# Nearest-neighbour upsampling on one core: two of the three loads move from SyncE to ScalarE

## The chip, the core and the metric

The kernel runs on one core of a Trainium2 chip. A core has several engines that run their own instruction streams and meet only through semaphores: TensorE, VectorE (DVE in the profile), ScalarE (ACT), GpSimd (POOL) and SyncE (SP). Data move between the chip's memory (HBM) and the core's own memory of 128 partitions by sixteen DMA engines. An engine issues a transfer, here SyncE or ScalarE, and the transfer's pieces are put on a hardware queue of that engine; the sixteen DMA engines work the queues off. In the profile q1 is the queue of SyncE and q10 that of ScalarE. The metric is the device time of one launch, in microseconds (us).

## The reference

The input `x` has 16 images of 64 channels of 64 x 64 floats (16.78 MB). Each pixel becomes a 2 x 2 block of the output, which has 16 x 64 x 128 x 128 floats (67.11 MB). Nothing is calculated; every number is copied four times.

```python
for i in range(new_h):
    for j in range(new_w):
        result[:, :, i, j] = x[:, :, i // scale_factor, j // scale_factor]
```

## The kernel before

All images and channels are laid end to end, which gives 65,536 rows of 64 floats. Each of the 128 partitions gets 512 consecutive rows, 128 KB. One tile, `mem`, holds a free part of 79 x 256 floats and behind it (from the index `WF` on) the 512 rows of the input, `xt`.

The input comes by three loads (line 195): rows 0 to 31, rows 32 to 287 and rows 288 to 511 of each partition, that is 8 KB, 64 KB and 56 KB in each partition, or 1024, 8192 and 7168 KB in all. Before the change all three are issued by SyncE, one after the other.

The output is made in nine groups of 54, 38, 54, 60, 54, 62, 64, 62 and 64 input rows. For each, VectorE copies the rows to a place in `mem` with each row twice and each float twice (`expanded`, line 215), and one DMA stores that place to HBM (line 217). The place alternates: even groups go to the start of `mem`, odd ones end where the group's own input rows begin, over input that is already used. A group can only be copied once the store that last read its place has landed. In the first group, row 0 is copied by an instruction of its own (line 214), which waits for the first load alone; the other 53 rows follow in a second copy, which waits for the second load. Groups 0, 1 and 8 are stored by SyncE, the others by ScalarE.

Semaphores and waits are put in by the framework. Two functions then edit the finished program. `begin_before_barrier` takes SyncE's first `EARLY` instructions out of the kernel's body, which must be loads that wait for nothing, and puts them into the opening part of the program, ahead of SyncE's first drain. That drain belongs to the opening barrier, at which all engines meet, so these loads start without waiting for the other engines. `close_early` edits the end: it lets GpSimd clear the semaphores early, and SyncE's last instruction waits for the last store. `close_on_gpsimd` is not used.

Of the kernel before, what the change touches and what calls it, by code (L numbers as in the profile page):

```python
# [6 lines left out]

EARLY = 3  # L10


def begin_before_barrier(nc):

    blocks = nc.main_func.blocks
    main, body = blocks[0], blocks[1]
    sp = mybir.EngineType.SP
    loads = [i for i in body.instructions if i.engine == sp][:EARLY]  # L20
    for load in loads:
        assert isinstance(load, mybir.InstDMACopy), type(load)
        assert not (load.sync_info and load.sync_info.on_wait)
    names = [i.name for i in loads]
    body.instructions = [i for i in body.instructions if i.name not in names]
    kept = list(main.instructions)
    at = next(
        n
        for n, i in enumerate(kept)
        if i.engine == sp and isinstance(i, mybir.InstDrain)  # L30
    )
    kept[at:at] = loads
    main.instructions = kept


def close_on_gpsimd(nc):
# [117 lines left out]
@with_exitstack  # L154
def kernel(
    ctx: ExitStack,
    tc: tile.TileContext,
    x: bass.AP,
    scale_factor: int,
    out: bass.AP,  # L160
):
    nc = tc.nc
    nc.at_finalize(begin_before_barrier)
    nc.at_finalize(close_early)
    P = nc.NUM_PARTITIONS
    s = int(scale_factor)
    B, C, H, W = x.shape
    R = B * C * H // P
    fdt = x.dtype

    xp = x.rearrange("b c h w -> (b c h) w").rearrange("(p r) w -> p r w", p=P)
    op = out.rearrange("b c (h hd) w -> (b c h) (hd w)", hd=s).rearrange(
        "(p r) w -> p r w", p=P
    )

    rows = [54, 38, 54, 60, 54, 62, 64, 62, 64]
    GROW = s * s
    FREE = 79
    WF = FREE * GROW * W
    assert sum(rows) == R
    mem_pool = ctx.enter_context(tc.tile_pool(name="mem", bufs=1))
    mem = mem_pool.tile([P, WF + R * W], fdt, name="mem")
    xt = mem[:, WF:].rearrange("p (r w) -> p r w", r=R)

    HEAD = 32
    cuts = [0, HEAD, R // 2 + HEAD, R]
    for lo, hi in zip(cuts, cuts[1:]):
        nc.sync.dma_start(out=xt[:, lo:hi], in_=xp[:, lo:hi])  # L195

    def expanded(r0, r1):
        return (
            xt[:, r0:r1].unsqueeze(2).unsqueeze(4).to_broadcast([P, r1 - r0, s, W, s])
        )  # L200

    r0 = 0
    before = (0, 0)
    for n, k in enumerate(rows):
        size = k * GROW * W
        at = 0 if n % 2 == 0 else WF + r0 * W - size
        assert at >= before[1] or at + size <= before[0]
        before = (at, at + size)
        u = mem[:, at : at + size].rearrange(
            "p (k a w b) -> p k a w b", k=k, a=s, w=W  # L210
        )
        k0 = 1 if n == 0 else 0
        if k0:
            nc.vector.tensor_copy(out=u[:, :k0], in_=expanded(r0, r0 + k0))  # L214
        nc.vector.tensor_copy(out=u[:, k0:], in_=expanded(r0 + k0, r0 + k))  # L215
        issuer = nc.sync if n in (0, 1, len(rows) - 1) else nc.scalar
        issuer.dma_start(out=op[:, r0 : r0 + k, :], in_=u)
        r0 += k
# [35 lines left out]
```

## Time and profile before

| | |
|---|---|
| time of the runs (median of 3) | 197.12 us (197.11 to 197.22) |
| span of the profiled execution, first to last instruction | 195.7 us |
| its own time, as far as the profile gives it | the span; the median of the runs is 1.4 us above it |
| VectorE busy | 76.9 us, 10 instructions |
| moved by DMA | 83.89 MB in 1728 packets |
| mean rate over the span | 429 GB/s |

The span counts from the first instruction to the last. A DMA is one instruction, but 144 packets here: eight rows of partitions and one small completion flag for each of the sixteen DMA engines, so that the 12 DMAs (three loads, nine stores) make 1728. A packet counts at its beginning in a view of short stretches, with all its bytes and all its time; in a stretch shorter than a packet, the DMA share and the rate can therefore be far above 1 and 430 or zero, while the mean over some packets is right. In the rows of such stretches stand: from and to, length, VectorE's busy time (with the number of instructions), GpSimd's, the TensorE clock, the DMA share and GB/s. Rows that begin with q1 or q10 give packets, MB and the share of the time of sixteen DMA engines. In the chain and in the timeline a row begins with start and duration in us. "SPq" and "ACTq" are the instructions by which SyncE and ScalarE issue, wait and meet at barriers.

### The profile page before, as it was taken

Reading aid. Unit: us, or ns where it says so; the run is one execution under the profiler, and the core shown is the slowest. Engines: PE = TensorE matmul, PEld = TensorE weight load, DVE = VectorE, ACT = ScalarE, POOL = GpSimd, SP = SyncE. Lnnn points to the kernel's source line nnn. Section 1 sums busy time; section 2 is a strip of 40 time slices with the busy share of each in tenths; the row PEclk is TensorE's granted clock in tenths of the full one; section 3 lists DMA queues with packets and bytes.
Section 4 is the critical chain, followed back from the end, with each engine's and each line's share of the span. In section 5 each row is a group of like instructions: output and inputs, shape, how many; then the busy total and the mean of one; then the engine's idle time right before and its main releaser. Section 6 shows DMA issues by size and latency. Waiting matters only on the chain.

```text
span 195.7 us, 76 instructions
## 1 busy us (share of the span) xinstructions
DVE 76.9 (39%) x10; POOL 0.2 (0%) x4
## 2 busy tenths in 40 slices
DVE  0000099990029287059008805920790079000000
POOL 0000000000000000000000000000000000000000
DMA  9999989989898988999999899999999999999994
GB/s 429 429 429 429 402 375 492 445 362 543 362 435 382 540 384 362 543 402 402 402 492 452 362 543 415 415 415 415 429 429 429 429 415 441 550 476 422 429 429 214
DMA packets 1728, 83.89 MB, mean 429 GB/s; under 512 B 192, under 2 KB 192, under 8 KB 192
## 3 DMA queue, kind: packets, MB, share of 16 engines
q10 hardware_dynamic: 864, 46.66, 55.0%
q1 hardware_dynamic: 864, 37.22, 44.3%
HBM read 16.78 MB, written 67.11 MB: 429 GB/s over the span
## 4 chain that ended last, share of the span: by engine, by line
DMA 61%; DVE 24%; SPq 0%; issue 0%
DMA out_dram<-mem 49%; DVE mem L215 24%; DMA mem<-in_x_dram 12%; SPq L195 0%
## 5 line engine op out<-in xcount | busy, mean ns | idle before, releaser
L215 DVE COPY mem<-mem 128x13824 f32<-128x13824 f32 (+5 forms) x9 | 76.6, 8515 | 84.6 <-DMA out_dram<-mem 65.5
L214 DVE COPY mem<-mem 128x256 f32<-128x256 f32 x1 | 0.3, 293 | 4.9 <-DMA mem<-in_x_dram 4.9
L235 POOL MEMSET const-bfloat16-1.0<- 128x1 bf16 x1 | 0.1, 101 | 0.0
L235 POOL MEMSET const-uint8-127<- 128x1 uint8 x1 | 0.1, 101 | 0.0
L235 POOL MEMSET const-float32-0.0<- 128x1 f32 x1 | 0.1, 98 | 0.2 <-issue 0.2
L235 POOL MEMSET const-float32-1.0<- 128x1 f32 x1 | 0.1, 98 | 0.0
## 6 DMA issues: line engine op xcount, KB each, us to landing
out_dram<-mem ACTq DMA_DIRECT2D x2, 7936.0 KB, 31.6
out_dram<-mem ACTq DMA_DIRECT2D x2, 6912.0 KB, 23.7
out_dram<-mem ACTq DMA_DIRECT2D x1, 7680.0 KB, 26.1
mem<-in_x_dram SPq DMA_DIRECT2D x1, 7168.0 KB, 40.2
out_dram<-mem SPq DMA_DIRECT2D x1, 6912.0 KB, 18.9
out_dram<-mem SPq DMA_DIRECT2D x1, 4864.0 KB, 25.1
mem<-in_x_dram SPq DMA_DIRECT2D x1, 1024.0 KB, 4.8
mem<-in_x_dram SPq DMA_DIRECT2D x1, 23.8
```

The lines of the kernel that those rows point to most:

```text
L214: nc.vector.tensor_copy(out=u[:, :k0], in_=expanded(r0, r0 + k0))
L215: nc.vector.tensor_copy(out=u[:, k0:], in_=expanded(r0 + k0, r0 + k))
L235: nc = _bacc.Bacc("TRN2", target_bir_lowering=False, num_devices=1)
```

## The change

The second and third load are issued by ScalarE instead of SyncE. `EARLY` becomes a table, one load for SyncE and two for ScalarE, and `begin_before_barrier` does for each of the two engines what it did for SyncE: it takes that many loads out of the body and puts them ahead of the engine's own drain in the opening part. Sizes, copies, stores and their queues, and the end of the program stay. The waits of copies and stores are on the same transfers as before.

```diff
-EARLY = 3
+EARLY = {mybir.EngineType.SP: 1, mybir.EngineType.Activation: 2}
...
     main, body = blocks[0], blocks[1]
-    sp = mybir.EngineType.SP
-    loads = [i for i in body.instructions if i.engine == sp][:EARLY]
-    for load in loads:
-        assert isinstance(load, mybir.InstDMACopy), type(load)
-        assert not (load.sync_info and load.sync_info.on_wait)
-    names = [i.name for i in loads]
-    body.instructions = [i for i in body.instructions if i.name not in names]
-    kept = list(main.instructions)
-    at = next(
-        n
-        for n, i in enumerate(kept)
-        if i.engine == sp and isinstance(i, mybir.InstDrain)
-    )
-    kept[at:at] = loads
-    main.instructions = kept
+    for engine, count in EARLY.items():
+        loads = [i for i in body.instructions if i.engine == engine][:count]
+        for load in loads:
+            assert isinstance(load, mybir.InstDMACopy), type(load)
+            assert not (load.sync_info and load.sync_info.on_wait)
+        names = [i.name for i in loads]
+        body.instructions = [i for i in body.instructions if i.name not in names]
+        kept = list(main.instructions)
+        at = next(
+            n
+            for n, i in enumerate(kept)
+            if i.engine == engine and isinstance(i, mybir.InstDrain)
+        )
+        kept[at:at] = loads
+        main.instructions = kept
...
     for lo, hi in zip(cuts, cuts[1:]):
-        nc.sync.dma_start(out=xt[:, lo:hi], in_=xp[:, lo:hi])
+        issuer = nc.scalar if lo else nc.sync
+        issuer.dma_start(out=xt[:, lo:hi], in_=xp[:, lo:hi])
```

## The prediction

> **What bounds the kernel now.** I read the page first, then the chain that ended last, then short stretches of the DMA traffic, since the page points there. Its queue part says that the two hardware queues, q1 (SyncE's) and q10 (ScalarE's), together took 55.0 + 44.3 = 99.3% of the time of all sixteen DMA engines over the span. VectorE, the only engine that computes, was busy for 39%.
>
> ```profile
> span 195.7 us, 76 instructions
> DVE 76.9 (39%) x10; POOL 0.2 (0%) x4
> q10 hardware_dynamic: 864, 46.66, 55.0%
> q1 hardware_dynamic: 864, 37.22, 44.3%
> HBM read 16.78 MB, written 67.11 MB: 429 GB/s over the span
> ```
>
> So the time is close to bytes over rate, and only a hole in the DMA traffic can lengthen it. The chain of waits shows where such a hole could come from: one load, the long first copy, the first store, and so on.
>
> ```profile
> 0.00 0.37 SPq L195
> 0.37 0.05 issue
> 0.42 23.76 DMA mem<-in_x_dram
> 24.19 0.02 issue
> 24.21 14.30 DVE mem L215
> 38.51 0.02 issue
> 38.52 18.93 DMA out_dram<-mem
> ```
>
> Call the three loads A (32 of the 512 image rows that a partition holds, 8 KB of it), B (256, 64 KB) and C (224, 56 KB), and the first store S0. B is seen landed at 24.2, VectorE copies until 38.5, S0 is issued at 38.52. Did the DMA engines run dry before S0? Packets are booked at the moment they begin and each DMA engine takes one partition's row at a time, so the traffic shows as waves of sixteen packets:
>
> ```profile
> 38.20:38.61 0.41, 0.38 (x2) 0.00 (x0) 1.00 5.18 2238
> 38.61:40.32 1.71, 1.71 (x1) 0.00 (x0) 1.00 0.00 0
> 40.32:40.73 0.41, 0.41 (x1) 0.00 (x0) 1.00 5.00 2158
> 40.73:42.36 1.63, 1.63 (x1) 0.00 (x0) 1.00 0.00 0
> 42.36:42.77 0.41, 0.41 (x1) 0.00 (x0) 1.00 4.98 2158
> ```
>
> The last column is GB/s booked. The wave at 38.20 is 2238 GB/s x 0.41 us = 0.92 MB, C's last rows (16 x 56 KB); the next at 40.32 is 0.88 MB, S0's first (16 x 54 KB). They are 2.12 us apart, and 0.92 MB / 2.12 us = 433 GB/s, the full rate: no hole. Two longer stretches, of one queue and of two, show nearly the same rate:
>
> ```profile
> 171.00:182.80 11.80, 0.00 (x0) 0.00 (x0) 1.00 0.99 428
> 58.00:68.00 10.00, 6.83 (x1) 0.00 (x0) 1.00 1.01 436
> ```
>
> **The change, part by part.** SyncE keeps A and loses two DMA issues; ScalarE gains those for B and C, ahead of its opening barrier. No byte, copy or store changes, nor which queue a store is on.
>
> *When B is issued.* Now it follows A on SyncE; then it is ScalarE's first work. The trace of before has ScalarE at its first instruction, the drain of the opening barrier, at 0.1 us.
>
> ```profile
> L235 ACTq DRAIN  x1: 8/8/8, 0.1 to 0.1; - x1
> L195 SPq DMA_DIRECT2D mem<-in_x_dram x3: 373/424/432, 0.0 to 0.9; - x3
> DMA to landing us min/median/max: 4.8/23.8/40.2
> 0.00 1.32 SPq L195 DMA_DIRECT2D mem<-in_x_dram  x3
> ```
>
> So B is issued at about 0.1 instead of 0.42, and C at about 0.1 + 0.42 + 0.05 = 0.6 instead of 0.9. That saves 0.3 us of issuing that lies on no path as long as A keeps the DMA engines busy: the engines start on A at 1.0, which is unchanged, and B only has to be there when they would run out.
>
> ```profile
> 0.50:1.00 0.50, 0.00 (x0) 0.00 (x0) 1.00 0.00 0
> 1.00:1.50 0.50, 0.00 (x0) 0.00 (x0) 1.00 1.97 279
> 1.50:2.00 0.50, 0.00 (x0) 0.00 (x0) 1.00 0.15 49
> 2.00:2.50 0.50, 0.00 (x0) 0.00 (x0) 1.00 0.89 360
> 4.00:4.50 0.50, 0.00 (x0) 0.00 (x0) 1.00 5.13 2212
> ```
>
> The burst at 4.00 to 4.50 is B's first wave (2212 x 0.5 = 1.1 MB), beginning as A's rows end. Term: 0.
>
> *The barrier.* SyncE reaches it 0.9 us sooner, ScalarE 0.9 us later (two issues of 0.42 to 0.43). What is behind it is VectorE's first copy, at 4.9 in before. Term: 0; the cover is over 3 us.
>
> *How A and B share the DMA engines.* This is the real content of the change. On one queue A went wholly ahead of B; on two queues they interleave. The trace shows how, where the last store (q1) joins the one before it (q10). First SyncE's store issues, the last of which ends at 38.52 + 128.19 = 166.71; then four stretches in order, each one wave long: 168.58 to 170.92, 170.92 to 173.33, 173.33 to 175.67, and 182.84 to 185.26.
>
> ```profile
> 38.52 128.19 SPq L217 DMA_DIRECT2D out_dram<-mem  x3
> ...
> q10 hardware_dynamic: 16, 1.02, 100.1%
> ...
> q1 hardware_dynamic: 16, 1.05, 100.3%
> ...
> q10 hardware_dynamic: 16, 1.02, 100.1%
> ...
> q1 hardware_dynamic: 16, 1.05, 100.0%
> q10 hardware_dynamic: 16, 0.00, 0.4%
> ```
>
> One row from one queue, one row from the other, at no loss of rate: 1.02 MB in 2.34 us is 436 GB/s. The last pair is the completion flags of q10 (16 packets of no size), which came only after one more wave of the other queue. Eight rows of A at 8 KB will then alternate with eight rows of B at 64 KB, and A, landed at 4.8 now, lands at about 21 to 24. The sum of A and B is the same, so B still lands at about 24.2. Only line 214's copy waits for A alone; it took 0.29 us.
>
> ```profile
> L214 DVE COPY mem<-mem 128x256 f32<-128x256 f32 x1 | 0.3, 293 | 4.9 <-DMA mem<-in_x_dram 4.9
> ```
>
> If A lands a wave ahead of B (A is issued first, and above, the wave of 168.58 is still q10's though the other store was issued by 166.71: an engine seems to have one more row of its current queue committed before it turns to the other), that copy stays hidden behind B's last wave. If they land together, it goes ahead of the long copy, which starts 0.29 + 0.02 = 0.31 us later, and S0 is issued at 38.83. S0's rows can begin 1.0 us after issue, as A's do on idle engines: 39.83, still before the engines finish C at 40.32. The slack is 40.32 - 38.52 - 1.00 = 0.80 us, so 0.31 costs nothing. Term: 0 either way; with the cover gone it would be the excess over 0.80.
>
> [...]
>
> *C beside the first stores.* C stays behind B on one queue. Now S0 queues behind C on q1; then it stands on another queue, and can alternate with C's last wave. C may land a wave (2 us) later. The first copy that reads its rows is the sixth of the nine, at 103.41, so nothing waits:
>
> ```profile
> 103.41 8.43 DVE L215 COPY mem<-mem 128x15872 f32<-128x15872 f32 x1 [10.83 <-DMA out_dram<-mem]
> ```
>
> SyncE's second store no longer has a load ahead of it either. From S0's landing on, the chain is the one of before. Term: 0.
>
> *The ramp.* This is the one unknown with a price. The first sixteen packets took long: 1.05 MB began at 1.0 and ended at 4.0 to 4.5, middle 4.25, where 1.05 MB / 434 GB/s = 2.4 us would do. The loss is 3.25 - 2.4 = 0.85 us. If B's long rows fill that gap, up to 0.85 us is gained. If two queues being set up at once delay A's rows, the nearest row is one issue, 0.42 us, lost. I take 0: between 1.5 and 2.0 only 49 GB/s began, on all engines at once, which looks like a first read's delay that any load pays, not like rows too short.
>
> Sum: 195.7 + 0 = 195.7 us of span. The runs' median is 197.12, 1.4 us above the span for what lies around it; I carry that over and forecast **197.1 us**. About 0.2%, 0.4 us, is what can be told from no change; the likely case by itself spans 196.8 to 197.5.
>
> **Rivals.**
>
> *A falls behind B, and S0 comes too late (slower).* If ScalarE's rows get ahead of SyncE's by the committed row, the order ends B's flag, first row of C, A's flag. A row of C is 2.12 us. A is then seen at 24.21 + 2.12 = 26.33, the long copy starts at 26.33 + 0.31 = 26.64, S0 is issued 14.3 us later at 40.95 and moves at 41.95. The engines ran dry at 40.32 to 40.73, middle 40.5: a hole of about 1.4 us, 198.5 us. One slow engine in sixteen is enough for the wait. For it: the slack is only 0.80 us, and A's lead over B is about 0.1 us. Against it: SyncE's issue is the first instruction in the span, and with the lead kept A lands early or together. It decides from 0.80 us of delay on. [...]
>
> *ScalarE's loads come late, so the change costs the cover that it counts on (slower).* If ScalarE's first DMA is slow to issue, the engines run out of A. They have A until 4.0; B, issued at 0.1, is due at 1.1. It decides from 2.9 us of lateness on and then costs 1 us per us; 198.1 for a further 1.0. Against it: ScalarE is at its barrier by 0.1 us.
>
> *The ramp is shortened (faster).* With two queues feeding each DMA engine, rows of 64 KB enter the 0.85 us gap. Half of it gives 196.7, all of it 196.3. For it: less than a third of the rate began between 1.0 and 2.0. Against it: the gap is common to all engines.
>
> **Chances.** No change, 0.62. A behind B, 0.18; ScalarE late or a slower start by more than 0.4 us, 0.08: slower, 0.26 in all. Ramp shortened by more than 0.4 us, 0.12: faster. The range runs from 196.7, half the ramp, to 198.5, A behind B; it leaves out the full ramp and what comes beyond a hole of 1.4 us, under 2 in 10.
>
> **What would show it.** Of the changed kernel: DMA traffic still starting at 1.0; A landing at some 20 to 24 us after issue in place of 4.8; the first short copy at 21 to 24.5; the long copy starting by 24.6 and S0 issued by 38.9; the wave after C's last one following at once at about 40.3. The forecast is wrong if the short copy begins after 24.9, if a stretch between 40 and 42 has no wave where one is due, or if the first 1.1 MB of traffic is done earlier.

## The result, and the profile after

The changed kernel takes 198.13 us (median, 198.10 to 198.31) against 197.12 us. The ratio is 1.0048, with an interval of 1.0036 to 1.0060: it is slower by 1.0 us. The profiled execution is the longest of these, with a span of 197.0 us against 195.7. The page of the changed kernel has the same bytes, packets and copies; only the split over the queues differs, as the two loads moved from q1 to q10.

```profile
span 197.0 us, 76 instructions
q10 hardware_dynamic: 1152, 62.39, 73.1%
q1 hardware_dynamic: 576, 21.50, 26.1%
```

The chain of waits of the changed kernel (start, duration, what) shows where the time came in. I keep the names of the prediction: loads A, B and C, first store S0.

```profile
0.12 24.54 DMA mem<-in_x_dram
...
24.67 14.30 DVE mem L216
...
38.99 19.70 DMA out_dram<-mem
...
58.71 7.37 DVE mem L216
...
66.10 20.34 DMA out_dram<-mem
```

B was seen landed at 24.19 and is now seen at 24.65: 0.46 us later, although it was issued 0.3 us sooner. S0 then took 19.70 us from its issue to its landing, where it took 18.93: another 0.77 us. Sum 1.23. From there on the pieces are those of before: the next copy took 7.37 us there too (57.48 to 64.85) and the next store 20.33, here 20.34. So there are two losses, both in the first 60 us.

**The first loss, at the start.** Short stretches of the changed kernel (last column: GB/s booked, as the packets begin):

```profile
1.00:1.50 0.50, 0.00 (x0) 0.00 (x0) 1.00 1.87 229
...
2.00:2.50 0.50, 0.00 (x0) 0.00 (x0) 1.00 0.70 164
...
3.00:3.50 0.50, 0.00 (x0) 0.00 (x0) 1.00 3.34 1442
3.50:4.00 0.50, 0.00 (x0) 0.00 (x0) 1.00 2.12 918
```

Data begin at 1.0 as before, but from 2.0 to 2.5 only 164 GB/s are booked where there were 360. The bursts between 3.0 and 4.0 hold B's first wave. The loss therefore falls before any row of B begins.

**The second loss, at the first store.** The stretches around C's end and S0's beginning, of the changed kernel:

```profile
38.50:39.10 0.60, 0.57 (x2) 0.00 (x0) 1.00 3.53 1529
...
40.60:41.25 0.65, 0.65 (x1) 0.00 (x0) 1.00 4.08 1361
...
42.85:43.15 0.30, 0.30 (x1) 0.00 (x0) 1.00 1.70 737
43.15:43.70 0.55, 0.55 (x1) 0.00 (x0) 1.00 0.23 101
43.70:44.00 0.30, 0.30 (x1) 0.00 (x0) 1.00 4.68 2028
```

C's last wave is booked from 38.50 on (1529 x 0.60 = 0.92 MB). S0's first wave follows 2.1 us later, at 40.60 (1361 x 0.65 = 0.88 MB), so it looks as if nothing were lost. But a row of S0 moves in 2.04 us, as the stretches of before show (40.32 to 42.36), and the second wave should start from 42.64 to 43.29. 737 x 0.30 = 0.22 MB, four rows, do about that; most of the others, 2028 x 0.30 = 0.61 MB or eleven rows, begin only after 43.70. On these DMA engines the first row of S0 was begun, and then lay for about 0.8 us: the first wave takes 4.08 x 0.65 = 2.65 us a row in the mean of all sixteen engines, 0.61 more than 2.04, and the loss is on twelve of the sixteen.

S0 was also ready later than the 1.0 us after issue that the prediction reckoned with. From 40.60 to 40.74 four DMA engines finish C (their completion flags, on q10), but one row of S0 begins (on q1):

```profile
q1 hardware_dynamic: 1, 0.06, 117.9%
q10 hardware_dynamic: 4, 0.00, 1.6%
```

Three engines thus had no row of S0 yet at 40.74, 1.75 us after its issue at 38.99.

Load A was seen landed at 17.4 instead of 4.8, ahead of B, and the short copy ran there, in time. The rival in which A falls behind B did not happen.

### The profile page after: what moved, and what is told of

Read it like the earlier page. It is cut to its first block, busy times and chain, and to the rows that moved or that the text cites. A ratio compares the mean times of both kernels' runs of the same rounds, so it can differ in the third digit from the quotient of the medians.

```text
span 197.0 us, 76 instructions
## 1 busy us (share of the span) xinstructions
DVE 76.9 (39%) x10; POOL 0.2 (0%) x4
## 3 DMA queue, kind: packets, MB, share of 16 engines
q10 hardware_dynamic: 1152, 62.39, 73.1%
q1 hardware_dynamic: 576, 21.50, 26.1%
## 4 chain that ended last, share of the span: by engine, by line
DMA 61%; DVE 24%; issue 0%
DMA out_dram<-mem 49%; DVE mem L216 24%; DMA mem<-in_x_dram 12%
## 5 line engine op out<-in xcount | busy, mean ns | idle before, releaser
L215 DVE COPY mem<-mem 128x256 f32<-128x256 f32 x1 | 0.3, 293 | 17.4 <-DMA mem<-in_x_dram 17.4
## 6 DMA issues: line engine op xcount, KB each, us to landing
mem<-in_x_dram SPq DMA_DIRECT2D x1, 1024.0 KB, 17.4
```

## The experiments

All times are medians; "before" is run beside each. The late start is read from the landing of B in the chain, the loss at S0 from S0's duration there (18.93 before, 19.70 in the changed kernel).

### B and C behind the barrier

```diff
-EARLY = {mybir.EngineType.SP: 1, mybir.EngineType.Activation: 2}
+EARLY = {mybir.EngineType.SP: 1}
```

> SyncE's load A stays ahead of the barrier, ScalarE's loads B and C are issued behind it, at about 0.8 us, when SyncE's issue is over. Set-up theory (the later start of all rows, 0.4 us, comes from two engines issuing their first loads at the same moment): B lands at 24.2 again and the first store S0 is issued at 38.5. For the hole of about 0.8 us at S0 there are two theories. Idle queue (a store put on a queue that stands idle while the other queue is busy takes about 2.8 us from issue to moving data): the hole stays, span 196.4, time 197.8 us. Lateness (S0 is only issued too late): with S0 back at 38.5 the hole goes, 197.1 us.

Measured: 197.93 us, ratio 1.0037 (1.0024 to 1.0050). From its chain:

```profile
0.78 23.41 DMA mem<-in_x_dram
...
38.52 19.72 DMA out_dram<-mem
```

B is issued at 0.78, 0.66 us later than in the changed kernel, and is seen landed at 24.18, 0.47 us sooner: the late start is gone. S0 is issued at 38.52 as in the kernel before, and still takes 19.72. Its stretches show the loss on all sixteen DMA engines:

```profile
40.32:40.73 0.41, 0.41 (x1) 0.00 (x0) 1.00 6.99 2158
...
42.36:42.77 0.41, 0.41 (x1) 0.00 (x0) 1.00 0.00 0
...
43.10:43.65 0.55, 0.55 (x1) 0.00 (x0) 1.00 3.71 1609
```

The first wave of S0 begins in the same stretch as before, but takes 6.99 x 0.41 = 2.87 us a row in place of 2.04. The second, due at 42.36, begins at 43.10 or later with all its 0.88 MB (1609 x 0.55). So the loss at S0 is not that S0 comes too late: lateness falls.

### S0 behind C on the same queue

```diff
-        issuer = nc.sync if n in (0, 1, len(rows) - 1) else nc.scalar
+        issuer = nc.sync if n in (1, len(rows) - 1) else nc.scalar
```

> The changed kernel, but S0 is issued by ScalarE, so that it stands behind load C on the same queue, as it did before the change (there on SyncE's). Idle queue: the hole at S0 goes, the later start stays: 197.5 us. Lateness: S0 is issued at 39.0 as in the changed kernel, the hole stays: 198.1 us.

and the same edit in the kernel before, whose loads are all SyncE's, so that S0 leaves C's queue there:

> The kernel before, but S0 is issued by ScalarE, whose queue is idle then, while load C ends on SyncE's. Idle queue: a hole of about 0.8 us after C's last rows, 197.9 us, with the start as before. Lateness: S0 is issued at 38.5 as before, no hole, 197.1 us.

Measured: 202.44 us (ratio 1.0267, 1.0251 to 1.0282) and 204.24 us (1.0356, 1.0339 to 1.0373). Neither theory said that. With S0 on one queue and the second store on the other, the two share the DMA engines (from 44 to 70 us of the first kernel 5.31 MB begin on q10 and 4.98 on q1), and S0 lands late. The chains of the first and the second:

```profile
39.06 26.07 DMA out_dram<-mem
```

```profile
38.53 28.39 DMA out_dram<-mem
```

The third group can be copied only when S0 has landed, and by then the queues have run out. In the first of the two kernels:

```profile
69.20:73.30 4.10, 4.07 (x2) 0.00 (x0) 1.00 0.00 0
```

Four us without a packet beginning. The times therefore decide nothing on S0's first rows, but the traces do. The stretch in which S0's sixteen first rows begin, in the first kernel and in the second:

```profile
40.50:41.25 0.75, 0.75 (x1) 0.00 (x0) 1.00 2.77 1180
```

```profile
40.40:40.75 0.35, 0.35 (x1) 0.00 (x0) 1.00 8.16 2528
```

DMA share times length is the mean time of a row here: 2.77 x 0.75 = 2.08 us with S0 behind C on one queue, although ScalarE issues both, and 8.16 x 0.35 = 2.86 us with S0 on the other queue, although SyncE issues all loads. The loss goes with S0's queue. To see this in the time, both stores have to move together, as is done further below.

### S0 issued somewhat sooner

```diff
-    rows = [54, 38, 54, 60, 54, 62, 64, 62, 64]
+    rows = [50, 38, 52, 60, 54, 64, 66, 64, 64]
```

> The changed kernel with a first group of 50 rows in place of 54 (the rows go to later groups), so that S0 is issued about 1.05 us sooner, at 37.9, some 2.7 us ahead of C's end in place of 1.6. Idle queue as a time to get going: the hole goes or falls under 0.2 us, 197.5 us. Idle queue as a fixed price of changing queues: the hole stays, 198.1 us. Lateness agrees with the first.

Measured: 197.88 us, ratio 1.0035 (1.0021 to 1.0048); the chain:

```profile
0.12 24.93 DMA mem<-in_x_dram
...
38.31 18.85 DMA out_dram<-mem
```

The time is inconclusive. In this execution B landed at 25.04, later still than in the changed kernel, so that S0 was issued at 38.31 and not at 37.9. S0 is smaller here (6400 KB against 6912), and its 18.85 us are not to be compared with the others. Its first rows can be: at 2.04 us for 54 KB a row of 50 KB would take 1.89. Six rows of S0 begin in the first of these stretches, the other ten in the second:

```profile
40.38:40.86 0.48, 0.48 (x1) 0.00 (x0) 1.00 2.14 640
40.95:41.60 0.65, 0.65 (x1) 0.00 (x0) 1.00 1.89 788
```

The six take 2.14 x 0.48 x 16 / 6 = 2.74 us each, the ten 1.89 x 0.65 x 16 / 10 = 1.97. So the loss is not on every DMA engine: those that ended C last, 2.6 us or more after S0's issue, are nearly free of it. Why is not shown.

### All three loads by ScalarE

```diff
-EARLY = {mybir.EngineType.SP: 1, mybir.EngineType.Activation: 2}
+EARLY = {mybir.EngineType.Activation: 3}
...
-        issuer = nc.scalar if lo else nc.sync
+        issuer = nc.scalar
```

> All three loads are issued by ScalarE ahead of the barrier; the stores stay as they are, so S0 goes to SyncE's queue, idle until then. Set-up theory: one engine issues alone, so A's rows and B start as in the kernel before (B seen landed at 24.2 to 24.4). Idle queue: S0 is issued at about 38.6 and its first rows move about 0.8 us late on most DMA engines: 197.9 us. If ScalarE's loads were slow in themselves, B would land at 24.6 as in the changed kernel and the time would be 198.3.

Measured: 198.08 us, ratio 1.0049 (1.0031 to 1.0067).

```profile
0.54 23.75 DMA mem<-in_x_dram
...
38.63 19.77 DMA out_dram<-mem
```

B is seen landed 0.10 us later than before (24.29), because ScalarE's first issue is at 0.12. It needs 23.75 us, before it needed 23.76. ScalarE's loads are not slow in themselves. The loss at S0 is there in full.

### S0 issued far sooner

```diff
-        k0 = 1 if n == 0 else 0
+        k0 = HEAD if n == 0 else 0
```

> The changed kernel, but the first short copy takes all 32 rows of load A in place of one, so that it runs while B is still arriving and S0 is issued some 8 us sooner, at about 31, far ahead of C's end. Idle queue as a time to get going (2.8 us): no late first rows of S0, since the queue has time to start beside C; the later start of all rows stays: 197.5 us. Idle queue as a fixed price of changing queues: the hole stays, 198.1 us.

and the same with B and C behind the barrier:

> As the kernel before this one in the list, and B and C are issued behind the barrier. Set-up theory and idle queue as a time to get going together: neither term is left, and with two of three loads on ScalarE the time is that of the kernel before, 197.1 to 197.2 us. If something else in having loads on ScalarE costs, more than that.

Measured: 199.94 us (ratio 1.0162, 1.0106 to 1.0218) and 200.20 us (1.0166, 1.0120 to 1.0213), with a wide spread of 199.58 to 201.88 over both; the profiled execution of the first is its slowest, 201.88. Both theories were wrong on the time. S0 was issued some 11 us sooner, and so stood beside four waves of C or more. The chains' rows of S0, of the first and of the second kernel:

```profile
27.85 34.41 DMA out_dram<-mem
```

```profile
27.33 32.82 DMA out_dram<-mem
```

S0 lands at 62.26 and at 60.15, before the change at 57.45, with the same bytes moved by then (three loads and S0). So 2.7 us are lost in the second kernel, which has no late start, while rows of C and of S0 alternate. The 4.8 us of the first kernel are more than that and its late start together, and what the rest is stays open. The first time that rows of C and of S0 change, in the first kernel:

```profile
29.60:30.70 1.10, 1.10 (x1) 0.00 (x0) 1.00 2.87 834
...
32.60:34.00 1.40, 0.48 (x1) 0.00 (x0) 1.00 1.57 632
```

A wave of C (834 x 1.10 = 0.92 MB) starts at 29.60 to 30.70 and would be over at 31.7 to 32.8; the next wave, S0's first, comes at 32.6 to 34.0, about 1 us late. This spoke for a price of the change from a load to a store on another queue, which starting sooner does not take away. But the price is not paid at every change. In the second kernel, the wave of C at whose end S0 comes in, the next wave of C, and the third after that first one:

```profile
29.70:30.20 0.50, 0.50 (x1) 0.00 (x0) 1.00 6.95 1835
35.00:36.20 1.20, 0.00 (x0) 0.00 (x0) 1.00 1.93 765
...
43.60:45.20 1.60, 0.00 (x0) 0.00 (x0) 1.00 1.34 573
```

A row of C takes 6.95 x 0.50 = 3.48 us, then 1.93 x 1.20 = 2.32, then 1.34 x 1.60 = 2.14; alone it takes 2.12. Half of the 2.7 us is lost where the two first meet, and then the loss fades.

### S0 four us ahead of C's end

To have one change only, S0 has to be in time and yet meet no more than C's last wave. B and C stay behind the barrier, and:

```diff
-        k0 = 1 if n == 0 else 0
+        k0 = 9 if n == 0 else 0
```

> B and C issued behind the barrier, as in the first run of this study, and the short copy takes 9 rows in place of 1, so that the long copy has 45 rows and S0 is issued at about 36.4, 4 us ahead of C's end in place of 1.8. Time to get going (an idle queue beside a busy one needs 2.8 us from issue): S0 is ready in time, its first row follows C's last one, no rows are late, 197.1 to 197.2 us. Change from load to store (a price of about 0.8 us on each DMA engine where rows of a load on one queue are followed by rows of a store on the other, whatever the lead): late rows at C's last or S0's first wave all the same, 197.9 us.

Measured: 198.21 us, ratio 1.0052 (1.0036 to 1.0068). S0's row of the chain, and the stretches:

```profile
36.36 22.54 DMA out_dram<-mem
```

```profile
38.20:38.61 0.41, 0.41 (x1) 0.00 (x0) 1.00 7.86 2238
...
40.32:41.19 0.87, 0.87 (x1) 0.00 (x0) 1.00 0.00 0
41.19:41.90 0.71, 0.40 (x1) 0.00 (x0) 1.00 2.71 1168
41.90:42.30 0.40, 0.00 (x0) 0.00 (x0) 1.00 0.32 138
```

C's last wave starts at 38.20, as in the kernel before. The next wave is due at 40.32 and comes at 41.19 to 42.30: this time it is C's last rows that lie, each about 1 us. The time to get going falls. With a lead of 1.8 us (first experiment) or of 4 us, the change costs 0.8 to 1.1 us per DMA engine.

There is one more rival, a fixed price of beginning on an idle queue. The kernel before can answer it. Its third store is the first work of ScalarE's queue and follows the second store, which is on SyncE's. Its sixteen first rows begin here:

```profile
68.10:68.60 0.50, 0.00 (x0) 0.00 (x0) 1.00 4.10 1770
```

They take 4.10 x 0.50 = 2.05 us each, as rows of 54 KB do alone: no loss from store to store. From load to load there was none either: in the first experiment B followed A on a queue not used before, and was seen landed at 24.18, in the kernel before at 24.19. The loss was seen only where both the queue and the direction change.

### Both first stores by ScalarE

In the changed kernel, and then in the kernel before:

```diff
-        issuer = nc.sync if n in (0, 1, len(rows) - 1) else nc.scalar
+        issuer = nc.sync if n == len(rows) - 1 else nc.scalar
```

> The changed kernel with the first two stores both issued by ScalarE, so that S0 stands behind C and the second store behind S0, all on one queue (S0 alone on ScalarE's queue let the two stores share the DMA engines, S0 landed late and the engines ran dry near 69 us). Idle queue: no late rows at S0, no dry stretch near 69; only the later start is left: 197.5 us. Lateness: 198.1 us.

> The kernel before, all loads on SyncE, but the first two stores both issued by ScalarE, so that they follow each other on one queue while load C ends on the other. Either theory of the hole: all sixteen DMA engines move S0's first rows about 0.8 us late and nothing else changes: 197.9 us. If the hole is bound to SyncE's queue or to loads issued by ScalarE: no hole, 197.1 us.

Measured, in the changed kernel: 197.94 us, ratio 1.0040 (1.0024 to 1.0056). S0 follows C on one queue:

```profile
0.12 24.69 DMA mem<-in_x_dram
...
39.16 18.96 DMA out_dram<-mem
```

S0 takes 18.96 us, 0.03 from the 18.93 of before: its loss is gone. The late start is left (B at 24.81, 0.62 us late), and another 0.20 us come after 93 us, in two stores that take 27.11 and 29.37 us (27.00 and 29.28 before). The time was expected at 197.5.

In the kernel before: 197.94 us, ratio 1.0037 (1.0024 to 1.0050).

```profile
0.41 24.02 DMA mem<-in_x_dram
...
38.78 19.74 DMA out_dram<-mem
```

Here S0 takes 19.74 us with all loads on SyncE. The loss at S0 can thus be made in the kernel before, by its queue alone, and taken away in the changed one, by its queue alone. (B landed 0.25 us later in this profile than in the first one of before, with nothing changed there; so much varies from launch to launch.)

### Load B 0.4 us later

```diff
-        kept[at:at] = loads
+        kept[at:at] = pauses + loads
```

where `pauses` are twelve drains that wait for nothing, on ScalarE only.

> The changed kernel with twelve empty drains on ScalarE ahead of its loads, so that B is issued some 0.3 us later, when SyncE's issue of A (0.38 us) is about over, and still ahead of the barrier. Overlap of issuing as the cause of the later start: with B issued from 0.38 us on, B is seen landed at 24.2 to 24.3 and only the hole is left, 197.9 us. Reading of B's rows beside A's as the cause: B lands at 24.6 to 24.8 as in the changed kernel, 198.1 us or more.

Measured: 197.91 us, ratio 1.0036 (1.0023 to 1.0049).

```profile
0.53 23.57 DMA mem<-in_x_dram
...
38.43 19.81 DMA out_dram<-mem
```

Issued at 0.53 in place of 0.12, B is seen landed at 24.10 in place of 24.65. So the late start is there when the two issues overlap (B's from 0.12, A's until 0.38) and gone with B's from 0.53. Load A landed ahead of B's first rows here (the short copy began at 4.77), so the run does not tell whether it is the issuing or B's reading, held back with it, that delays A. That A is already behind from 2.0 to 2.5 us in the changed kernel, before a row of B begins, speaks against the rows of B. Over all profiles with load A the two cases do not overlap: B is seen landed at 24.65 to 25.04 in the seven in which both engines issue at once, and at 24.10 to 24.44 in the nine others.

### No small load ahead

The kernel before with two loads:

```diff
-EARLY = 3
+EARLY = 2
...
-    cuts = [0, HEAD, R // 2 + HEAD, R]
+    cuts = [0, R // 2 + HEAD, R]
```

> The kernel before with two loads in place of three: rows 0 to 287 in one, no small load A ahead. Ramp as a delay of the first read that any load pays: B still lands at 24.1 to 24.2, time 197.1 us. Ramp as the price of short rows: up to 0.7 us sooner, down to 196.4 us.

Measured: 197.71 us, ratio 1.0023 (1.0013 to 1.0033): slower. B's row of the chain:

```profile
0.00 24.47 DMA mem<-in_x_dram
```

The rows are seen landed 0.28 us later than with the small load, and the short copy (0.29 us) now stands in the chain too. So short rows are not the price of the ramp; it is paid with long ones too. Whether it is more then is not shown by this profile: B's landing varied by 0.25 us above with nothing changed in the loads.

### Both losses undone

Two of three loads stay on ScalarE, behind the barrier, and the first two stores go to ScalarE. Beside it, on the same chip, the late start alone and the changed kernel once more:

```diff
-EARLY = {mybir.EngineType.SP: 1, mybir.EngineType.Activation: 2}
+EARLY = {mybir.EngineType.SP: 1}
...
-        issuer = nc.sync if n in (0, 1, len(rows) - 1) else nc.scalar
+        issuer = nc.sync if n == len(rows) - 1 else nc.scalar
```

> A is issued by SyncE ahead of the barrier, B and C by ScalarE behind it, and the first two stores by ScalarE, behind C on its queue. The two terms as the whole loss: B is seen landed at 24.2, S0's rows follow C's at 40.3 without late ones, 197.1 to 197.2 us, with two of three loads still on ScalarE. A third cost of loads on ScalarE: 197.4 us or more.

> The later start alone (the changed kernel with the first two stores on ScalarE, as in an earlier run, which gave 197.94). If the start's price varies from launch to launch, B is seen landed between 24.5 and 24.9 and the time lies between 197.5 and 198.0; if 197.94 was typical, 197.9.

> The changed kernel as it is. If the terms overlap because each hits only some of the DMA engines and the slowest one sets the end: 198.0 to 198.2, less than the sum of the two terms measured alone (0.8 + 0.7).

Measured: 197.11 us, ratio 0.9997 (0.9987 to 1.0006), for both undone; 197.86 us, 1.0034 (1.0020 to 1.0047), for the late start alone; 198.36 us, 1.0059 (1.0046 to 1.0073), for the changed kernel. The chain with both undone:

```profile
0.78 23.39 DMA mem<-in_x_dram
...
38.51 19.09 DMA out_dram<-mem
```

B at 24.17, S0 19.09: both as before, and so is the time. The two losses are the whole of it; having loads on ScalarE costs nothing else that can be measured. Together (1.0 and 1.24 us in two comparisons) they cost less than the sum of what each costs alone, 0.74 and 0.74 to 0.85. In part this is no overlap: in both runs with the late start alone 0.20 us come from later stores (27.11 and 29.37 us in each), which the changed kernel does not have (26.95 and 29.30). In the repeat the loss at S0 was on four DMA engines only (from 43.60 to 44.20 second rows of 0.22 MB begin, 369 GB/s x 0.60 us), in the first run on twelve, in the run with B and C behind the barrier on all sixteen; the slowest one sets the end (S0 still took 19.56 us in the repeat). I read it so that DMA engines which the late start has put out of step are hit less often, but no run isolates that.

## Why the prediction was wrong

**The frame held.** No change was forecast, 197.1 us, and 198.13 were measured. The time is bytes over rate (in the changed kernel too the two queues take 73.1 + 26.1 = 99.2% of the DMA engines' time), and only a hole in the DMA traffic could lengthen it. That the later barrier is worth nothing, that C and the short copy have no reader in a hurry, and that the chain is unchanged after S0's landing, all show in the profile after. B's earlier issue gained nothing, as the prediction said, but it was not free: issued 0.4 us later, B landed in time (24.10).

**"Term: 0" for the ramp was mis-sized.** The prediction named the possibility, two queues set up at once, and its price, one issue of 0.42 us, and took 0. The profiles show 0.46 to 0.85 us at B's landing (24.65 to 25.04, against 24.19), and the two runs with S0 behind C 0.74 and 0.85 us in the time, of which 0.20 us come later. The argument for 0, that a delay common to all DMA engines must be a first read's, was beside the point: a delay that any load pays can still grow, here by 0.46 to 0.85 us.

**"S0's rows can begin 1.0 us after issue ... Term: 0" failed in another way than its rival.** The slack of 0.80 us was used to show that S0 is in time. The 1.0 us in it is too short, as three engines had no row of S0 1.75 us after its issue, but that cost these some 0.2 us (by 40.84 seven engines had finished C and six had begun S0), and S0's first wave began at 40.60, right behind C's. (The 1.0 us runs from the beginning of A's issue; from its end, at 0.37, it is 0.63.) The step that failed is the next part, "C beside the first stores", where S0's stand on another queue than C's was costed at nothing. The evidence quoted for two queues alternating without loss was of two stores. The row of a load followed by the row of a store on the other queue was not in the trace of before at all, and should have been bounded and not been read off from stores. It costs 0.74 us in the time by itself. The signs named for S0 did not show it: the short copy began at 17.4, and a wave came at 40.60. The wave that was missing is the next one, due from 42.64. What holds the row up inside the DMA engine stays open.

**The rival "A falls behind B"** gave nearly the right time, 198.5, by the wrong mechanism: A landed at 17.4, ahead of B. It is luck that the range, whose upper end is this rival's time, holds the measured one. The estimate of 20 to 24 for A was off because four rows of A per DMA engine (64 in all) had gone when B's first wave had come, by 4.0 us, and only the other four alternated with B's.

**Two queues, one set of DMA engines.** The rows of both queues run on the same sixteen DMA engines: from 5.5 to 6.5 us of the changed kernel sixteen rows of A (q1) and sixteen of B (q10) begin. The prediction costed the second queue at nothing beyond that; measured, the same bytes cost 0.77 us more at S0 when load and store stood on two queues, and 0.46 us more at B's landing when two engines issued at the same moment.

## What to carry to other kernels

Where a stream of loads ends and a stream of stores begins and DMA is the bound, put the first store on the queue of the last load; on the other queue the change cost 0.7 us here with the store issued 1.8 us ahead of the loads' end, and not less with 4 or 13 us. Two queues of stores alternated without loss (a wave of 1.02 MB in 2.34 us, 436 GB/s, in the kernel before), so evidence from one pair of transfers is not evidence for another. A wave of packets that begins in time is not yet a wave that moves: look at when the next one begins (here S0's first wave began at 40.60, right behind C's, and most of its second after 43.70 in place of 42.64).

## What the runs showed of the hardware that was not expected

- Rows of a load and of a store on two queues lost time where they first met, and less and less afterwards: 2.7 us over the load C and S0 in the run with S0 issued at 27.33 and B behind the barrier, 1.36 of them in the first wave (3.48 us for a row of 2.12).
- A queue that was freshly fed beside a busy one waited long for its first turn: B, issued at 0.12, had its first rows at 3.0 to 4.0; with B issued at 0.53 or 0.78 the rows of A, then busy, all went ahead of it (the short copy, which waits for A, began at 4.77 and 4.87). S0 had no row yet on three DMA engines 1.75 us after its issue, where A's first rows came 1.0 us after theirs.
- The copy's rate went with the number of rows, odd or even. In the run with all of A's rows copied first, 32 and 22 rows go at 1.85 and 1.82 elements per ns:

```profile
L215 DVE COPY mem<-mem 128x8192 f32<-128x8192 f32 x1 | 4.4, 4427 | 17.5 <-DMA mem<-in_x_dram 17.5
L216 DVE COPY mem<-mem 128x5632 f32<-128x5632 f32 x1 | 3.1, 3094 | 2.8 <-DMA mem<-in_x_dram 2.8
```

  The 53 rows of the kernels before and after take 14.3 us (13568 elements, 0.95 per ns), and 45 rows, in the run with S0 four us ahead, 12.16 us (11520 elements, 0.95 per ns). In all runs the odd numbers of rows went at about half the rate of the even ones: 0.95 per ns also for 49 rows (12544 elements in 13.23 us, the run with a first group of 50), 0.90 for 9 (2304 in 2.55, the run with S0 four us ahead), and 1.82 to 1.89 for even numbers from 22 to 66. Why is not shown. In the kernel before it held up no row: the long copy ended at 38.51, and C's last rows at 40.32.
